# Token-major values in the gMLP and in the shared K/V, and a later start of FFN2's forms, in a one-core decoder step

## The chip, the cores and the metric

The kernel runs on one core of one Trainium2 chip, as one program. The metric is device time in microseconds: the median of three runs of the kernel before is 2067.21 us (2066.38 to 2067.87).

## The reference

One inference step of a two-layer decoder: 512 prompt tokens and 32 sample tokens (8 sequences of 4), model width 1024, everything in float32. Layer A mixes tokens with a gMLP, layer B with attention; the keys, the values and the forget gates of layer B come from layer A's output once ("shared K/V"). The parts that the change touches:

```python
def gmlp_mix(xn, w_in, v_norm, w_s, b_s, w_out):
    u, v = jnp.split(xn @ w_in, 2, axis=-1)
    v = rmsnorm(v, v_norm)
    ...
    s = jnp.einsum('gts,bnsgd->bntgd', ws, vg)      # per chunk of 128 tokens and group of 128 features
    s = s + b_s[:, :c].T[None, None, :, :, None]
    return (u * s) @ w_out, v                       # v of the sample tokens is an output

def shared_kv(h, kv_norm, w_kvf, b_f, k_norm):
    kvf = rmsnorm(h, kv_norm) @ w_kvf
    k = rmsnorm(kvf[..., :D_ATT].reshape(bsz, L, N_HEADS, HEAD_DIM), k_norm)
    v = kvf[..., D_ATT:2 * D_ATT].reshape(bsz, L, N_HEADS, HEAD_DIM)
    logf = jax.nn.log_sigmoid(kvf[..., 2 * D_ATT:] + b_f)
    return k, v, logf
```

Around these stand, in each layer, FFN1, the mixer, FFN2 and a gated per-layer embedding (PLE), each with its own rmsnorm and residual sum.

## The kernel before

Activations lie feature-major: a tile is 128 features by 544 tokens (512 of the prompt, then the 32 samples), eight such chunks make the width 1024. The order of the stages is FFN1, gMLP, FFN2, PLE, shared K/V, FFN1, attention, FFN2, PLE.

**Products.** float32 accuracy comes from fp32r matmuls: each operand is split into hi and lo, and three products are summed, hi·hi, hi·lo and lo·hi (L235, L239, L241 in `mm`, each in two matmuls of 256 and 288 columns). `tile_mm` makes one tile of 128 features by 544 tokens: the weights are the stationary operand, the activations the moving one, eight chunks of the contraction, 24 pairs of matmuls. Weights come in pieces of 512 KB in the order that `build` lists them: SP loads a piece (L159), ScalarE (ACT) casts it to hi (L192), VectorE (DVE) subtracts to get lo (L193), a few pieces ahead of their use. An activation is split in the same way by `prep` (L291 on ScalarE with the norm's gain, L292 on VectorE) or by `split_pair` (L279, L280). A norm's factor per token, rstd, is multiplied in after the product, when VectorE empties PSUM. A PSUM tile `ps` is two banks, and there are three; `pb` is one bank, and there are two. Each chunk of the residual that is complete calls `on_chunk`, which prepares the next stage's input (`next_norm`): the split, the sum of squares (a Square on ScalarE, L318, an add on GpSimd, L320), and, for the first pairs of chunks of a following FFN, `forms`, the sums and differences of blocks that the FFN's seven-product scheme multiplies (L301 twice on ScalarE; L305, L307, L308 on VectorE; two splits, L279 and L280). `early` says for how many pairs: 3 ahead of FFN2 of layer A, 2 ahead of FFN2 of layer B.

**gMLP.** Eight tiles of v are made feature-major, then eight of u. The spatial product wants v with tokens on the partitions, so `v_turn` multiplies by the norm and transposes a tile on TensorE (L612 four blocks of the prompt, L613 the samples) and ScalarE copies it back. `spatial` is plain fp32 (L623 the prompt, L626 the samples).

**Shared K/V** (`kv`). First the forget gates' tile, then eight tiles of k, then eight of v. A head's k norm needs the sum of squares over its 128 features: `head_stat` (L710) sums with a matmul of ones, heads 0 to 3 in one burst after head 5's tile and heads 4 to 7 in one burst after the first v tile; the chain of rsqrt follows on VectorE (L337, L340, L341), its rows go to DRAM (L721), come back to all partitions (`tmp<-rows`, L726), and `k_norm` (L784) multiplies. Each v tile is multiplied by rstd on VectorE (L765), stored, transposed on TensorE (L796, L797 in this stage's `v_turn`), split and written to DRAM for attention.

**Attention's end.** After the heads, the output is projected: first the tokens of the first half (`project_half`), then the second half, a chunk of 128 features at a time, with all eight heads in the contraction (`project`, L1172, L1175, L1176 in `product`; L1196 adds to the residual). Each of the eight `project` steps ends with `on_chunk`.

**Order.** The order within an engine is set by a scheduler from the program's order and the dependencies; in attention a list written by hand (`ORDER`) gives the program's order. ScalarE and VectorE run their instructions strictly in the order of their queue, and SP issues nearly all DMAs.

## Time and profile before

| | |
|---|---|
| median of 3 runs | 2067.21 us |
| the profiled execution | 2068.19 us |
| its span, first to last instruction | 2066.4 us |
| mean granted clock of TensorE | 0.999 |
| TensorE busy | 2042.8 us, 99% |
| VectorE busy | 1509.9 us, 73% |
| ScalarE busy | 941.1 us, 46% |
| GpSimd busy | 180.5 us, 9% |
| data moved | 237.94 MB, 115 GB/s on the mean |

A row of a timeline reads: start (us from the span's start), duration, engine, line, operation, the tile written and the tiles read, shape, how many instructions the row holds, and in brackets the idle time just before and what ended it. A matmul's duration includes its way through the array, so the pace of TensorE is read from one start to the next. A plain fp32 matmul leaves two records, an fp32r one leaves one.

### The profile page before, as it was taken

What the parts mean: (1) busy time and instruction counts of PE and PEld (TensorE: products, weight loads), DVE (VectorE), ACT (ScalarE), POOL (GpSimd) and SP (SyncE); (2) the same over time, 40 slices, a digit from 0 to 9 for tenths busy, and PEclk for the clock granted to TensorE, in tenths of its full rate; (3) what the DMA queues carried; (4) which work ended last, traced back from release to release, by engine and by line L of the source; (5) the groups of instructions that cost most, each with busy time, mean ns of one, the idle gap of its engine ahead of it and who ended that gap; (6) DMA issues with size and microseconds to landing.
All of it is one profiled execution on the core that took longest, in us unless ns stands there. A gap on an engine that the chain in (4) does not pass through costs nothing.

```text
span 2066.4 us, 38759 instructions
## 1 busy us (share of the span) xinstructions
PE 2042.8 (99%) x16388; PEld 2015.9 (98%) x16388; DVE 1509.9 (73%) x1874; ACT 941.1 (46%) x1389; POOL 180.5 (9%) x230
## 2 busy tenths in 40 slices
PE   8999999999999999999999999999999999999999
PEld 8999999999999999999999999999987999999999
DVE  7877777556687778776698777786476878777773
ACT  6535344423554344454356344444374744344451
POOL 0000000400100000052050000001042200000020
PEclk9999999999999999999999999999999999999999
DMA  5233234212223232432184322323668332232421
GB/s 184 83 111 110 74 105 146 92 45 82 83 92 113 72 113 79 147 98 92 35 321 168 102 103 93 113 74 121 214 209 287 103 103 82 103 103 82 129 97 44
DMA packets 93887, 237.94 MB, mean 115 GB/s; under 512 B 9602, under 2 KB 27554, under 8 KB 93714
## 3 DMA queue, kind: packets, MB, share of 16 engines
q1 hardware_dynamic: 93570, 235.42, 33.9%
q8 instruction: 129, 2.11, 0.4%
q14 instruction: 44, 0.36, 0.1%
q10 hardware_dynamic: 144, 0.04, 0.0%
HBM read 218.94 MB, written 16.49 MB: 114 GB/s over the span
## 4 chain that ended last, share of the span: by engine, by line
PE 93%; DVE 3%; DMA 1%; ACT 1%; issue 1%; POOL 1%; SPq 0%; ACTq 0%; DVEq 0%; POOLq 0%
PE ps L485 33%; PE ps L235 16%; PE ps L241 16%; PE ps L239 16%; PE pb L485 6%; PE ps L1172 1%; PE ps L1176 1%; DVE big L193 1%; PE ps L1175 1%; ACT big L192 0%; PE ps L1129 0%; DMA tmp<-rows 0%; PE ps L623 0%; PE pb L1091 0%; POOL big L837 0%
## 5 line engine op out<-in xcount | busy, mean ns | idle before, releaser
L485 PE MATMUL ps<-big,big 128*128 128x272 f32 x5616 | 727.2, 288 | 0.7 <-DVE big L502 0.7
L485 PEld LDWEIGHTS ps<-big,big 128*128 128x128 f32 x5616 | 714.2, 189 | 0.9 <-issue 0.9
L193 DVE TENSOR_TENSOR big<-big,big 128x1024 fp32r<-128x1024 f32 (+2 forms) x538 | 590.1, 1099 | 108.8 <-ACT big L192 108.2
L192 ACT CAST big<-big 128x1024 fp32r<-128x1024 f32 (+2 forms) x538 | 488.4, 932 | 265.1 <-DVE big L178 260.4
L235 PE MATMUL ps<-big,big 128*128 128x256 f32 (+1 forms) x2832 | 590.5, 290 | 8.0 <-ACT big L192 7.3
L241 PE MATMUL ps<-big,big 128*128 128x256 f32 (+1 forms) x2832 | 585.1, 288 | 1.0 <-DVE big L193 1.0
L239 PE MATMUL ps<-big,big 128*128 128x256 f32 (+1 forms) x2832 | 585.0, 287 | 0.0
L235 PEld LDWEIGHTS ps<-big,big 128*128 128x128 f32 x2832 | 454.1, 189 | 10.3 <-ACT big L192 7.3
L239 PEld LDWEIGHTS ps<-big,big 128*128 128x128 f32 x2832 | 457.1, 189 | 0.0
L241 PEld LDWEIGHTS ps<-big,big 128*128 128x128 f32 x2832 | 453.4, 188 | 2.5 <-DVE big L193 2.1
L320 POOL TENSOR_TENSOR st<-st,tmp 128x544 f32<-128x544 f32 (+1 forms) x63 | 88.3, 1401 | 1619.2 <-ACT tmp L318 1619.0
L524 DVE SCALAR_TENSOR_TENSOR big<-ps,big 128x544 f32<-128x544 f32 x160 | 115.6, 723 | 106.6 <-PE ps L241 106.4
L178 DVE TENSOR_TENSOR big<-big,big 128x1024 f32<-128x1024 f32 x156 | 190.1, 1219 | 0.0
L493 ACT COPY tmp<-ps 128x544 f32<-128x544 f32 x117 | 71.7, 613 | 147.4 <-PE ps L485 147.4
L448 ACT ACTIVATE big<-big 128x544 f32<-128x544 f32 x88 | 58.0, 660 | 161.9 <-DVE big L445 160.7
L485 PE MATMUL pb<-big,big 128*128 128x272 f32 x936 | 124.0, 288 | 0.0
L445 DVE TENSOR_TENSOR big<-big,st 128x1088 f32<-128x1088 f32 x88 | 113.4, 1290 | 10.6 <-ACT big L507 8.9
L485 PEld LDWEIGHTS pb<-big,big 128*128 128x128 f32 x936 | 120.2, 189 | 0.0
L291 ACT ACTIVATE big<-big,gains 128x544 fp32r<-128x544 f32 (+1 forms) x80 | 56.0, 704 | 119.0 <-DVE big L524 64.9
L280 DVE TENSOR_TENSOR big<-big,big 128x544 fp32r<-128x544 f32 (+1 forms) x104 | 75.2, 726 | 28.3 <-ACT big L279 28.0
L292 DVE SCALAR_TENSOR_TENSOR big<-big,gains,big 128x544 fp32r<-128x544 f32 (+1 forms) x80 | 63.9, 805 | 26.6 <-ACT big L291 26.6
L279 ACT CAST big<-big 128x544 fp32r<-128x544 f32 (+1 forms) x104 | 66.7, 645 | 29.0 <-DVE big L784 15.2
(187 smaller groups left out, 1246.2 us busy)
## 6 DMA issues: line engine op xcount, KB each, us to landing
big<-in_w SPq DMA_DIRECT2D x156, 512.0 KB
big<-in_w2a SPq DMA_DIRECT2D x64, 512.0 KB
big<-in_w2b SPq DMA_DIRECT2D x32, 384.0 KB
big<-in_w13p SPq DMA_DIRECT2D x16, 512.0 KB
big<-in_win SPq DMA_DIRECT2D x16, 512.0 KB
big<-in_wg SPq DMA_DIRECT2D x16, 512.0 KB
big<-in_wkv SPq DMA_DIRECT2D x16, 512.0 KB
big<-in_ck SPq DMA_DIRECT2D x16, 512.0 KB
```

What stands on the lines that cost most here:

```text
L178: self.nc.vector.tensor_tensor(t, a, b, ALU.add if op == "+" else ALU.subtract)
L192: self.nc.scalar.copy(hi, src)
L193: self.nc.vector.tensor_tensor(lo, src, hi.bitcast(F32), ALU.subtract)
L235: i = nc.tensor.matmul(out[:, a:b], wh, xh[:, a:b], start=s, stop=False)
L239: nc.tensor.matmul(out[:, a:b], wh, xl[:, a:b], start=False, stop=False)
L241: nc.tensor.matmul(out[:, a:b], wl, xh[:, a:b], start=False, stop=e)
L280: self.nc.vector.tensor_tensor(pair[:, 1, cols], src, pair[:, 0, cols].bitcast(F32), ALU.subtract)
L320: nc.gpsimd.tensor_tensor(acc[:, cols], acc[:, cols], sq, ALU.add)
L445: tt(g, g, rstd.unsqueeze(1).broadcast_to([P, 2, T]), ALU.mult)
L485: nc.tensor.matmul(dst[w], a[:, c], b, start=k in "152" and kp == 0 and n == 0, stop=kp == NKP - 1 and n == 2, skip_group_check=True)
L493: nc.scalar.copy(t["r" + k], t["C" if k == "5" else "A"])
L524: nc.vector.scalar_tensor_tensor(h[c], whole(out), 0.5, h[c], ALU.mult, ALU.add)
```

## The change

In the gMLP the prompt's v and in the shared K/V the prompt's v are made token-major at once. `token_half` takes a block of 128 tokens as the stationary operand and the weights' hi and lo as the moving one, 512 columns (features, four heads) at a time. The weights are laid out anew (`wgv`, `wv`): a piece is two chunks of the contraction by 512 features, four pieces make a half, and a piece is 4 blocks of tokens x 2 chunks x 3 products = 24 matmuls of 512 columns (L603, L604, L605). A half's result is two `ps` tiles, held over four pieces. The transposes on TensorE are gone.

The 32 sample tokens are done apart: `raw_sample` scales them by the gain, and plain fp32 matmuls with the raw weights (L611), four chunks of the contraction beside each other in 32 columns of the array each, give four partial sums stacked on the 128 partitions; `sample_sums` (L617) adds the four with one matmul of a 0/1 matrix. `columns` (L578, L580) turns rstd from a row into a column per token, eight small fp32 matmuls.

In the gMLP a half is copied out of PSUM by ScalarE, which also sums the squares; the norm's factor becomes a small column (`v_norm`), and VectorE multiplies it in. In the shared K/V ScalarE empties a half with rstd as its scale (L848, eight activations a half; L851 the samples'), and the steps of k, v, the statistics (L788), the norms (`k_norm`, now L896), the next stage's `prep` and `forms` follow a list, `KV_ORDER`. v's outputs change layout, and the host puts them back in order.

`early` becomes a map from the chunk after which `forms` runs to the pair: the same as before ahead of FFN2 of layer A, and ahead of FFN2 of layer B after chunks 5 and 6 instead of 1 and 3.

The lines of helpers move: L192, L193 become L198, L199; L279, L280 become L285, L286; L291, L292 become L297, L298; L305, L307, L308 become L311, L313, L314; L318 becomes L324; L337, L340, L341 become L343, L346, L347; L1196 becomes L1294.

VectorE in the shared K/V, around the end of the rsqrt chain of heads 4 to 7 (L341, L347). Before (L784 is the norm of heads 0 and 1, on `big_11000`, which L280 then splits; L877, L879, L880, L888 belong to the forget gates):

```order
L340 SCALAR_TENSOR_TENSOR tmp_11542<-pb_11532,tmp_11542 128x272
L877 TENSOR_SCALAR sm_12131<-sm_12044,consts 128x8
L280 TENSOR_TENSOR big_11560<-big_11000,big_11560 128x512
L341 SCALAR_TENSOR_TENSOR st_11541<-tmp_11542,st_11541 128x544
L879 SCALAR_TENSOR_TENSOR sm_12131<-sm_12044,consts,sm_12131 128x8
L292 SCALAR_TENSOR_TENSOR big_11566<-big_86,gains,big_11566 128x544
L879 SCALAR_TENSOR_TENSOR sm_12131<-sm_12044,consts,sm_12131 128x8
L193 TENSOR_TENSOR big_11570<-big_11399,big_11569 128x1024
L765 TENSOR_TENSOR tmp_11627<-ps_11578,st_10926 128x544
L784 SCALAR_TENSOR_TENSOR big_11000<-big_11000,gains,tmp_11462 128x544
```

Now (L896 is the norm, `big_11007` holds heads 4 and 5, `big_11208` heads 6 and 7):

```order
L343 SCALAR_TENSOR_TENSOR tmp_11312<-st_11311 128x544
L346 SCALAR_TENSOR_TENSOR tmp_11312<-pb_11301,tmp_11312 128x272
L346 SCALAR_TENSOR_TENSOR tmp_11312<-pb_11302,tmp_11312 128x272
L347 SCALAR_TENSOR_TENSOR st_11311<-tmp_11312,st_11311 128x544
L896 SCALAR_TENSOR_TENSOR big_11007<-big_11007,gains,tmp_11372 128x544
L896 SCALAR_TENSOR_TENSOR big_11007<-big_11007,gains,tmp_11374 128x544
L286 TENSOR_TENSOR big_11412<-big_11007,big_11412 128x512
L896 SCALAR_TENSOR_TENSOR big_11208<-big_11208,gains,tmp_11416 128x544
L298 SCALAR_TENSOR_TENSOR big_11418<-big_87,gains,big_11418 128x544
L896 SCALAR_TENSOR_TENSOR big_11208<-big_11208,gains,tmp_11476 128x544
L199 TENSOR_TENSOR big_11422<-big_11328,big_11421 128x1024
```

The norms of heads 4 to 7, which read the chain's rows back from DRAM into `tmp`, now stand right behind the chain; before, the norms of heads 1 to 3 stood between.

ScalarE at the same place now (L285 splits head 4, `big_11007`, L297 prepares a chunk for FFN1, L198 splits v's piece 5, L848 empties the first PSUM tile, `ps_11109`, of the first half of v):

```order
L285 CAST big_11412<-big_11007 128x512
L297 ACTIVATE big_11418<-big_87,gains 128x544
L198 CAST big_11421<-big_11328 128x1024
L848 ACTIVATE big_11458<-ps_11109,sm_10827 128x2x128
L848 ACTIVATE big_11459<-ps_11109,sm_10827 128x2x128
L848 ACTIVATE big_11458<-ps_11109,sm_10827 128x2x128
L848 ACTIVATE big_11459<-ps_11109,sm_10827 128x2x128
L848 ACTIVATE big_11458<-ps_11110,sm_10827 128x2x128
```

The split of piece 5 and the emptying of the first half stand behind the split of a head whose norm waits for the round trip.

ScalarE in attention's last projections. Before (L192 splits the weights of `project`, L301 and L279 belong to `forms`, L291 and L318 to `on_chunk`):

```order
L301 ACTIVATE big_18680<-big_86,gains 128x544
L291 ACTIVATE big_18473<-big_87,gains 128x272
L279 CAST big_18685<-tmp_18683 128x544
L318 ACTIVATE tmp_18728<-big_87 128x272
L279 CAST big_18686<-tmp_18684 128x544
L192 CAST big_18695<-big_18613 128x1024
L291 ACTIVATE big_18492<-big_87,gains 128x272
L318 ACTIVATE tmp_18765<-big_87 128x272
L192 CAST big_18732<-big_18648 128x1024
L301 ACTIVATE big_18768<-big_87,gains 128x544 x2
```

Now:

```order
L198 CAST big_18240<-big_18170 128x1024
L297 ACTIVATE big_17995<-big_87,gains 128x272
L324 ACTIVATE tmp_18236<-big_87 128x272
L198 CAST big_18277<-big_18207 128x1024
L198 CAST big_18314<-big_18244 128x1024
L297 ACTIVATE big_18014<-big_87,gains 128x272
L324 ACTIVATE tmp_18273<-big_87 128x272
L307 ACTIVATE big_18350<-big_86,gains 128x544 x2
```

The forms of pair 0 (L307 at the end) now stand behind the last weight splits of `project`.

The core of the diff:

```diff
+KV_ORDER = """
+k0 k1 c0 k2 k3 k4 s0 k5 r0 r1 v0 n0 r2 k6 n1 r3 k7 n2 p0 s1 v1 n3 p1 r4 r5 v2 n4 r6 p2 v3 n5 r7 p3 f0
+v4 n6 w0 p4 v5 n7 w0 p5 v6 f1 p6 v7 p7 w0 w0
+"""
...
-    def next_norm(self, h, gcol, early=0):
+    def next_norm(self, h, gcol, early={}):
...
-            if c % 2 and c // 2 < early and cols.stop == T:
-                box["f"].append(self.forms(h, gcol, c // 2, self.pairs(box)))
+            if c in early and cols.stop == T:
+                box["f"].append(self.forms(h, gcol, early[c], self.pairs(box)))
...
+    def raw_sample(self, h, gcol, x):
+        for c in range(NC_):
+            self.nc.gpsimd.tensor_scalar(x[:, c, :], h[c][:, SEQ:], self.gain(gcol + c), None, ALU.mult)
+        return x
+    def columns(self, rstd):
+        nc, t = self.nc, self.pb()
+        for j in range(4):
+            nc.tensor.matmul(t[:, j:j + 1], rstd[:, j * P:(j + 1) * P], self.ident[:, 0:1], start=True, stop=True)
+        for j in range(4):
+            nc.tensor.matmul(t[32 * j:32 * j + 32, 4:5], rstd[:, SEQ:], self.ident[:, 0:1], start=True, stop=True,
+                             skip_group_check=True)
+        rc = self.sm(5)
+        nc.scalar.copy(rc, t[:, 0:5])
+        return rc
+    def token_half(self, xs, xraw, half, u):
+        nc = self.nc
+        hi, lo = self.unit()
+        raw = self.raws[self.pieces[self.p_next - 1]["src"][0]]
+        self.advance()
+        if u == 0:
+            half["p"] = self.ps(), self.ps()
+            half["r"] = []
+        half["r"] += [raw[:, 0:512], raw[:, 512:1024]]
+        for i in range(4):
+            t, out = slice(i * P, i * P + P), half["p"][i // 2][:, i % 2, :]
+            for a in range(2):
+                k, c = 2 * u + a, slice(512 * a, 512 * a + 512)
+                xh, xl = xs[k]
+                nc.tensor.matmul(out, xh[:, t], hi[:, c], start=k == 0, stop=False)
+                nc.tensor.matmul(out, xh[:, t], lo[:, c], start=False, stop=False)
+                nc.tensor.matmul(out, xl[:, t], hi[:, c], start=False, stop=k == NC_ - 1)
+        if u % 2:
+            if u == 1:
+                half["s"] = self.pb()
+            for n in range(4):
+                k = 2 * u - 2 + n
+                nc.tensor.matmul(half["s"][32 * n:32 * n + 32, :], xraw[:, k, :], half["r"][k], start=k < 4, stop=k >= 4,
+                                 skip_group_check=True)
+    def sample_sums(self, sv, half):
+        t = self.pb()[:NS, :]
+        self.nc.tensor.matmul(t, self.c[:, C_SUM:C_SUM + NS], sv[:, 512 * half:512 * half + 512], start=True, stop=True)
+        return t
 
...
-        rstd, sq, v = None, self.st(), []
-        for c in range(NC_):
-            if rstd is None:
-                p, rstd = self.tile_rstd(xs, box["acc"])
-            else:
-                p = self.tile_mm(xs)
-            if c % 2 == 0:
-                vt = self.big()
-
-            def take(p=p, vc=vt[:, c % 2, :]):
-                nc.vector.tensor_tensor(vc, whole(p), rstd, ALU.mult)
-                self.ssq(sq, vc, first=not v)
-                v.append(vc)
-            self.evac(take)
+        gvr = self.big()[:, 0:2, :512]
+        nc.sync.dma_start(out=gvr[:NS], in_=i["gvrow"].partition_broadcast(NS).rearrange("p o (a n) -> p (o a) n", a=2))
+        xraw = self.raw_sample(h, G_MIX, self.ks)
+        ss, v, sv = self.sm(10), [], self.flat(1024)
+        nc.vector.memset(ss, 0.0)
+        for g in range(2):
+            half = {}
+            for u in range(4):
+                self.token_half(xs, xraw, half, u)
+                if (g, u) == (0, 1):
+                    rstd = self.rstd(box["acc"])
+                if (g, u) == (0, 3):
+                    rc = self.columns(rstd)
+            for a, p in enumerate(half["p"]):
+                x = self.flat(1024).rearrange("p (i d) -> p i d", i=2)
+                v.append(x)
+                nc.scalar.copy(x, p)
+                for n in range(2):
+                    k = 4 * a + 2 * n + g
+                    nc.scalar.activation(self.tmp()[:, :512], p[:, n, :], AF.Square, accum_out=ss[:, k:k + 1])
+            nc.scalar.copy(sv[:, 512 * g:512 * g + 512], half["s"])
...
-        def v_turn(c):
...
-            for j in range(4):
-                nc.tensor.transpose(t[:, 0, j * P:(j + 1) * P], v[c][:, j * P:(j + 1) * P], self.ident)
-            nc.tensor.transpose(t[:NS, 1, :P], v[c][:, SEQ:], self.ident)
...
+        def v_scale(g):
+            for a in range(2):
+                x, f = v[2 * g + a], rv[:, 2 * a:2 * a + 2]
+                nc.vector.tensor_tensor(x, x, f.unsqueeze(2).broadcast_to([P, 2, 512]), ALU.mult)
...
+        def v_step(n):
+            g, u = divmod(n, 4)
+            self.token_half(xs, xraw, half, u)
+            if u < 3:
+                return
+            rc = box["rc"]
+            vs = [self.flat(1024).rearrange("p (h i d) -> p h i d", h=2, i=4) for _ in range(2)]
+            for i in range(4):
+                for a in range(2):
+                    nc.scalar.activation(
+                        vs[a][:, :, i], half["p"][i // 2][:, i % 2, 256 * a:256 * a + 256].rearrange(
+                            "p (h d) -> p h d", h=2), AF.Copy, scale=rc[:, i:i + 1])
+            nc.scalar.activation(sv[:, 512 * g:512 * g + 512], half["s"], AF.Copy, scale=rc[:, 4:5])
+            box["v"] = [(4 * g + a, vs[a // 2][:, a % 2].rearrange("p i d -> p (i d)")) for a in range(4)]
...
+        def norm(hh):
+            with self.tc.issue_after(box["last"].ins):
                 self.k_norm(hh, kraw, rows)
...
+        do = dict(k=k_tile, v=v_step, w=v_store, c=cols, s=stats, r=row, n=norm, p=prep, f=forms)
+        for step in KV_ORDER.split():
+            do[step[0]](int(step[1:]))
...
-        on, nxt = self.next_norm(h, G_FFN2, early=3)
+        on, nxt = self.next_norm(h, G_FFN2, early={1: 0, 3: 1, 5: 2})
...
-        on, nxt = self.next_norm(h, G_FFN2 + 8, early=2)
+        on, nxt = self.next_norm(h, G_FFN2 + 8, early={5: 0, 6: 1})
```

More of the change, by code (lines that the diff above doesn't have):

```diff
@@ L646, in gmlp @@
         u_tile(0)
[L647 removed]
+        rv, vs = v_norm()
+        v_scale(0)
         u_tile(1)
+        sample_scale()
         u_tile(2)
[L650 to L654 removed]
+        for c, spatials in ((3, (0,)), (4, (1,)), (5, (2, 3)), (6, (4, 5)), (7, (6, 7))):
             u_tile(c)
[L656 to L657 removed]
+            if c == 3:
+                v_scale(1)
             spatial(*spatials)
@@ L743, in kv, with k_tile, take @@
         sqs, bcs, rows = [], [], {}
-        for hh in range(NH):
+        nxt = {"x": {}, "f": []}
+        box, half, sv = {}, {}, self.flat(1024)
+        xraw = self.small.tile([P, NC_ * NS], F32, tag="xraw", name="xraw", bufs=1)[:].rearrange("p (c t) -> p c t", t=NS)
+        self.raw_sample(h, G_KV, xraw)
+        def k_tile(hh):
             p = self.tile_mm(xs)
             if hh % 2 == 0:
-                kt = self.big()
-            def take(p=p, kc=kt[:, hh % 2, :]):
-                nc.vector.tensor_tensor(kc, whole(p), rstd, ALU.mult)
+                box["k"] = self.big()
+            def take(p=p, kc=box["k"][:, hh % 2, :]):
+                box["last"] = nc.vector.tensor_tensor(kc, whole(p), rstd, ALU.mult)
                 kraw.append(kc)
@@ L753, in kv @@
             self.evac(take)
-            if hh == 5:
-                bcs += self.head_rows(sqs[:4])
-            if hh >= 6:
-                rows[hh - 6] = bcs[hh - 6]()
-        vpend = None
-        nxt = {"x": {}, "f": []}
-        for hh in range(NH):
-            p = self.tile_mm(xs)
-            if hh == 0:
-                bcs += self.head_rows(sqs[4:])
-            vc = self.tmp()
-            last = nc.vector.tensor_tensor(vc, whole(p), rstd, ALU.mult)
-            nc.sync.dma_start(out=o["v"][hh], in_=vc)
-            if vpend is not None:
-                self.v_turn(*vpend)
-            vpend = (hh, vc)
-            with self.tc.issue_after(last.ins):
-                self.k_norm(hh, kraw, rows)
-            if hh + 2 < NH:
-                rows[hh + 2] = bcs[hh + 2]()
-            nxt["x"][hh] = self.prep(h[hh], ffn_gain + hh)
-            if hh in (3, 5):
-                nxt["f"].append(self.forms(h, ffn_gain, len(nxt["f"]), self.pairs(nxt)))
@@ new lines, in v_store, with cols, stats, row @@
+        def v_store(_):
+            for hh, x in box["v"][:2]:
+                pair = self.big(F32R)
+                nc.sync.dma_start(out=o["v"][hh], in_=x)
+                self.split_pair(pair, x, slice(0, SEQ))
+                nc.sync.dma_start(out=self.vd[hh], in_=pair[:, :, :SEQ].bitcast(F32))
+            del box["v"][:2]
+        def cols(_):
+            box["rc"] = self.columns(rstd)
+        def stats(a):
+            bcs.extend(self.head_rows(sqs[4 * a:4 * a + 4]))
+        def row(hh):
+            rows[hh] = bcs[hh]()
@@ L778, in kv @@
+        for a in range(2):
+            nc.scalar.copy(vs[:, a, :], self.sample_sums(sv, a))
+        nc.sync.dma_start(out=o["vs"].rearrange("t (a n) -> t a n", a=2), in_=vs)
+        nc.sync.dma_start(out=self.vsd[:].rearrange("t (a n) -> t a n", a=2), in_=vs)
         return nxt, rstd
@@ L1219, in build @@
         self.ffn_pieces(0)
-        plain([i["win"][NC_ + c] for c in range(NC_)] + [i["win"][c] for c in range(NC_)])
+        plain([i["wgv"][c] for c in range(NC_)] + [i["win"][c] for c in range(NC_)])
         plain(i["wout"][c] for c in range(NC_))
@@ L1223, in build @@
         ple_units(0)
-        plain([i["wf"]] + [i["wkv"][c] for c in range(2 * NC_)])
+        plain([i["wf"]] + [i["w" + x[0]][int(x[1])] for x in KV_ORDER.split() if x[0] in "kv"])
         self.ffn_pieces(2)
```

82 lines of the change are left out of this document (41 added, 41 removed).

## The prediction

> **What bounds the kernel now.** I read the page's busy times first, then the waits of TensorE, then timelines of the places that the change touches. The page's row on TensorE, and four rows of its waits (engine, line, what it waited for: us in total, times, longest):
>
> ```profile
> PE 2042.8 (99%) x16388; PEld 2015.9 (98%) x16388; DVE 1509.9 (73%) x1874; ACT 941.1 (46%) x1389; POOL 180.5 (9%) x230
> PE ps L235 <- ACT big L192: 7.3, 1, 7.3
> PE ps L241 <- DVE big L193: 1.0, 2, 0.5
> PE pb L797 <- DVE big L280: 0.5, 1, 0.5
> ```
>
> TensorE sets the end; 7.3 us of its idle time is the first weights' arrival, which nothing here touches. So the change is worth what it takes from TensorE's own work, plus the waits that it removes and makes. The sum is made against the profiled execution (2068.19 us, span 2066.4) and set on the median of the runs, 2067.21; 0.2%, about 4.1 us, is what a measurement of this kernel can tell from no change.
>
> **The products of the prompt.** A tile of eight chunks was 24 pairs of matmuls (256 and 288 columns); a token-major half is four pieces of 24 matmuls of 512 columns. A pair's pace stands between two L235 rows that are 168 pairs apart, the other's between the first and the last of five rows of attention, of which four matmuls of 512 columns lie between:
>
> ```profile
> 345.13 0.41 PE L235 MATMUL ps<-big,big 128*128 128x256 f32 x2
> ...
> 386.94 0.41 PE L235 MATMUL ps<-big,big 128*128 128x256 f32 x2
> 1514.90 0.40 PE L1012 MATMUL ps<-big,big 128*128 128x512 f32 x1
> ...
> 1515.83 0.27 PE L1020 MATMUL ps<-neg,identr 128*128 128x256 f32 x1
> ```
>
> 41.81 / 168 = 0.249 us for a pair, 0.93 / 4 = 0.2325 us for 512 columns. Each of the two stages (gMLP's v, the shared v) had 192 pairs, 47.8 us, and gets 192 matmuls, 44.6 us: together **-6.3**.
>
> **The transposes** go: eight groups of five in each stage.
>
> ```profile
> 446.95 0.60 PE L612 MATMUL ps<-consts,big 128*128 128x128 f32 x4
> 447.38 0.27 PE L613 MATMUL ps<-consts,big 128*32 128x128 f32 x1
> 447.49 0.60 PE L612 MATMUL ps<-consts,big 128*128 128x128 f32 x4
> ```
>
> 447.49 - 446.95 = 0.54 for five, so 16 x 0.54 = **-8.6**.
>
> **The 32 sample tokens** now cost plain fp32 matmuls of 512 columns, four beside each other in the columns of the array. The nearest work is the paged attention's L1129 (same shapes), one group alone and then two in a row:
>
> ```profile
> 1578.44 0.29 PE L1175 MATMUL ps<-big,big 128*128 128x272 f32 x1
> 1578.66 1.05 PE L1129 MATMUL ps<-big,tmp 128*32 128x512 f32 x4
> 1579.64 0.39 PE L1176 MATMUL ps<-big,big 128*128 128x272 f32 x1
> 1579.87 0.29 PE L1172 MATMUL ps<-big,big 128*128 128x272 f32 x1
> ...
> 1583.93 1.92 PE L1129 MATMUL ps<-big,tmp 128*32 128x512 f32 x16
> 1585.78 1.06 PE L1134 MATMUL ps<-big,tmp 32*32 32x512 f32 x8
> ```
>
> The neighbours of the first group are half a pair, 0.125 us, apart when nothing lies between; here 1.43 us hold two such steps, so a group alone takes 1.43 - 0.25 = 1.18 us. Eight instructions in a row leave 16 records (each fp32 instruction leaves two) and take 1.85, with 0.25 for going in and out 2.1. gMLP's order has four groups apart: 4.7. The shared KV's has 8, 6 and 2 instructions together: 2.1 + 2.1 + 1.2 = 5.4. Together **+10.1**. `sample_sums` (L617) has no row: one instruction of 512 columns alone. A group's four run beside each other, so I price a single one like a group; below that the bound is half. Two in a row in gMLP 2.0, two apart in KV 2.4: **+4.4** (2.2 to 4.4).
>
> **The columns of rstd** (L578, L580): four fp32 matmuls with a stationary of 128 columns and four of 32, each moving one column. The spatial products of 128 columns and the samples' of 32 bound them:
>
> ```profile
> 489.81 1.95 PE L623 MATMUL ps<-big,big 128*128 128x128 f32 x16
> 491.69 0.63 PE L626 MATMUL ps<-tmp,big 32*128 32x32 f32 x4
> 492.25 0.52 PE L235 MATMUL ps<-big,big 128*128 128x256 f32 x2
> ```
>
> 0.12 a record at most (1.88 / 16) and 0.14 with the way out included (0.56 / 4): 16 records are at most 1.9; I put them at 1.3, since one column streams nothing, and the lowest at 0.6. Twice: **+2.6** (1.2 to 3.8). The Trainium skill, "TensorEngine Tiling (Array Packing)", section Instruction Overhead, has a matmul of one column cost as much as one of 60, about 60 cycles; sixteen of them would be an estimated 0.4 us, and the sum 1.8 us lower. No run here shows a one-column matmul.
>
> **The heads' statistics.** Before, the sums of squares of heads 4 to 7 were one burst; the new order has four pairs, each between other products, since the k tiles of heads 5 to 7 now have v pieces between them. A single pair (attention) and the burst:
>
> ```profile
> 1475.66 0.28 PE L241 MATMUL ps<-big,big 128*128 128x256 f32 x1
> 1475.86 1.10 PE L710 MATMUL pb<-tmp,ones 128*32 128x272 f32 x4
> 1476.90 0.40 PE L241 MATMUL ps<-big,big 128*128 128x288 f32 x1
> ...
> 1030.42 0.41 PE L241 MATMUL ps<-big,big 128*128 128x256 f32 x2
> 1030.76 1.12 PE L710 MATMUL pb<-tmp,ones 128*32 128x272 f32 x16
> 1031.81 0.52 PE L235 MATMUL ps<-big,big 128*128 128x256 f32 x2
> ```
>
> Next to 0.125 us without it, the pair costs 1476.90 - 1475.66 - 0.125 = 1.11, the burst 1031.81 - 1030.42 - 0.25 = 1.14. So 4 x 1.11 - 1.14 = **+3.3**.
>
> **Waits of the shared KV.** The three of 0.5 us above (L241 twice, L797) lie in this stage, behind a VectorE that multiplied every v tile by rstd; that work is now ScalarE's, so **-1.5**. One wait is new. VectorE's order now has k_norm of head 4 (L896) right behind the end of the rsqrt chain of heads 4 to 7, and k_norm needs the chain's result after a round trip through DRAM. ScalarE's split of head 4 waits for it, and behind that, strictly in order, stand the split of weight piece v5 and the evacuation of the first half's v, whose PSUM tile TensorE wants. Attention shows the whole trip (DVE's L341 ends the chain, SP's L721 writes rows, its L726 reads them back, L964 is the norm); the row ahead is KV's own write:
>
> ```profile
> 1037.97 1.14 SPq L721 DMA_DIRECT2D rows<-st  x4
> ...
> 1479.18 0.73 DVE L341 SCALAR_TENSOR_TENSOR st<-tmp,st 128x544 f32<-128x544 f32 x1
> 1479.97 1.14 SPq L721 DMA_DIRECT2D rows<-st  x4
> 1487.01 0.78 DVE L964 SCALAR_TENSOR_TENSOR big<-big,gains,tmp 128x544 f32<-128x544 f32 x1
> 1489.45 0.78 DVE L964 SCALAR_TENSOR_TENSOR big<-big,gains,tmp 128x544 f32<-128x544 f32 x1 [0.28 <-DMA tmp<-rows]
> ```
>
> ScalarE's steps from the groups of instructions (count | busy us, mean ns):
>
> ```profile
> L192 ACT CAST big<-big 128x1024 fp32r<-128x1024 f32 x378 | 391.4, 1047 | 265.1 <-DVE big L178 260.4 <-PE pb L485 2.1 <-ACT big L192 0.5
> L291 ACT ACTIVATE big<-big,gains 128x544 fp32r<-128x544 f32 x64 | 47.8, 750 | 98.2 <-DVE big L524 64.9 <-DVE big L661 17.4 <-DVE big L696 11.6
> L279 ACT CAST big<-big 128x512 fp32r<-128x512 f32 x16 | 9.9, 619 | 18.8 <-DVE big L784 15.2 <-DVE big L964 3.5
> ```
>
> Count from the end of the last statistic. To the write: 3.1 us in attention (1476.90 to 1479.97), 6.2 in KV (1031.81 to 1037.97, with other work between); I take 4.5. From the write to the first norm 7.0 at most, to the last 9.5; I take 6.0, as head 4's read is first in the queue. k_norm 0.8, split 0.6, next chunk's L291 0.75, v5's split 1.05: 13.7; the evacuation's first four activations, half the split's columns each, estimated 0.42: 15.4. TensorE's order has before that point 37 matmuls of 512 columns (8.6) and two of the samples' bursts (4.2): 12.8. So it waits 15.4 - 12.8, about **+2.5** (0 to 6). Before, the norms of heads 1 to 3 stood between chain and norm.
>
> What that does to the clock: in attention's tail, below, waits of 2.19 and 0.75 us were followed by a clock of 0.66. The Trainium skill, "TensorE: Matmul & The Clock Gate", section Why this matters for your kernels, allows idle gaps of up to about 3 us before the clock halves; this trace halved it with no gap over 2.19. By the rule a wait of 2.5 us costs no clock; by the row it may cost the 1.65 us worked out below, which I leave to the upper end.
>
> **Attention's tail.** The third and the fourth of the last eight projections waited, since `forms` for FFN2's pairs 0 and 1 stood ahead of weight splits on ScalarE and VectorE:
>
> ```profile
> 1617.59 0.29 PE L1176 MATMUL ps<-big,big 128*128 128x272 f32 x1
> 1620.06 0.39 PE L1172 MATMUL ps<-big,big 128*128 128x272 f32 x1 [2.19 <-ACT big L192]
> 1621.32 0.56 PE L1176 MATMUL ps<-big,big 128*128 128x272 f32 x1 [0.75 <-DVE big L193]
> 1624.84 0.29 PE L1176 MATMUL ps<-big,big 128*128 128x272 f32 x1
> ```
>
> The stretch's busy times by engine (PE, PEld, DVE, ACT, POOL), then the granted clock:
>
> ```profile
> 1620.00:1625.00 5.00, 4.19 (x19) 3.98 (x20) 4.82 (x7) 3.63 (x7) 0.99 (x1) 0.66 0.25 93
> ```
>
> From 1617.59 to 1624.84 are 18 steps of 0.125, 2.25 us: 5.0 were lost, of which 1.65 to the clock (15 steps from 1621.32 took 3.52). With the forms after chunks 5 and 6 every split stands ahead of them, and this goes. Late next is FFN2's start: its second and fourth weight pieces' lo now stand behind forms on VectorE; I count 1.0 lost (0 to 4). **-4.0**.
>
> **Sum:** -6.3 - 8.6 + 10.1 + 4.4 + 2.6 + 3.3 - 1.5 + 2.5 - 4.0 = **+2.5**: 2070.7 for the profiled execution, 2069.7 on the median. gMLP's own part is about nothing (-3.2 - 4.3 + 4.7 + 2.0 + 1.3 = +0.5), KV's about +6, attention's -4. In gMLP no new wait is counted: the evacuation by ScalarE (46% busy) of a half lies under the next half's 22 us; uncovered, a copy like L192's 1.05 and two squares like L279's 0.62 would cost 2.3 us for each PSUM tile.
>
> **The rivals.** (a) Slower: the KV's wait grows. Between KV's reads and writes the trip can be longer than attention's; if k_norm of head 4 comes 9.5 us behind the write, as the last of the four did, the wait is 6.0, and 1.65 of clock come on top: 2069.7 + 3.5 + 1.65 = 2074.9. It decides from a trip of about 7.6 us on, since 1.6 us more than forecast pass the 0.2%. For it: the norm's own queue, and ScalarE in strict order. Against it: head 4's read stands first in the queue. (b) Faster: the trip is over in time (wait 0), the tail's gain is whole, the columns cost 0.6 each and a lone L617 half a group: 2069.7 - 2.5 - 1.0 - 1.4 - 2.2 = 2062.6. For it: a lone fp32 matmul and a one-column one have no row here; against it: the dependent order on VectorE. (c) FFN2's start takes back all that the tail gains (+4.0 on the forecast, 2073.7): the forms need both chunks of a pair, so five more VectorE steps a pair fall into the first tiles. For it: VectorE has 4.82 of 5.00 us busy in the row above; against it: eight splits less ahead of them.
>
> **How the numbers follow.** Forecast 2069.7, no change that can be told: 0.40, of its own 2066 to 2072. (a) 0.22, (b) 0.25, (c) 0.13. From (b) most is faster by over 0.2%, from (a) and (c) nearly all slower: faster 0.24, same 0.41, slower 0.35. The range, 2061.5 to 2075.5, takes in (b) and (a).
>
> **What would show it.** Right: in the changed kernel's profile L611 bursts at 1.2 and 2.1 us, L617 at 1.0 to 1.2, single statistics at 1.1; in KV, VectorE's L896 waiting for DMA and TensorE's first 512-column matmul on the reused PSUM tile waiting for ScalarE's L848, for 1 to 5 us; no wait and a full clock in the last projections. Wrong: 512-column matmuls at another pace than 0.23, or a new wait over 3 us in gMLP or FFN2's start.

## The result and the profile after

| | before | changed |
|---|---|---|
| median of 8 runs | 2068.2 us | 2073.36 us |
| range of the runs | 2066.38 to 2069.22 | 2071.69 to 2074.93 |
| span of the profiled execution | 2066.4 us | 2069.9 us |

The ratio is 1.0028, 95% interval 1.0019 to 1.0037: 5.2 us slower between the medians, 3.9 to 7.7 by the interval. The forecast was 2.5 us slower, with 2061.5 to 2075.5 as its range. The profiled execution of the changed kernel is its fastest of the eight (2071.69), which is why the spans differ by 3.5 only.

To see where the time went I cut TensorE's rows at places that both kernels have: the first and the last matmul of each FFN's seven-product scheme (L485 before, L491 now) and the last matmul of attention's projection (L1175 before, L1273 now). Microseconds between the cuts, in the two kernels and in three of the experiments below:

| stretch | before | changed | forms only | gMLP only | K/V only |
|---|---|---|---|---|---|
| end of FFN1's products to start of FFN2's, layer A: gMLP | 220.3 | 219.4 | 220.3 | 219.4 | 220.3 |
| end of FFN2's products of A to start of FFN1's of B: PLE, shared K/V | 232.8 | 240.3 | 232.9 | 232.9 | 240.0 |
| FFN1's products of B | 306.5 | 306.5 | 306.5 | 306.5 | 306.5 |
| to the last projection: attention | 223.1 | 217.4 | 217.1 | 225.2 | 223.8 |
| to the end of FFN2's products of B | 331.1 | 334.2 | 334.2 | 331.2 | 331.2 |

The four other stretches agree to 0.1 us wherever the code is the same, and the changed K/V to 0.3 (240.3 and 240.0). Attention's moves by 2.1 us here between kernels that share all of its code, and by 3.3 over the experiments (216.3 in e7, 219.5 in e6), so a difference there counts only above that. Part of it is the clock: the last projections of "gMLP only" have the waits of before (2.18 and 0.75 us), but the clock is halved behind them for 6.8 us, where before had 3.4, and that alone is 1.7 us. A row has the stretch, its length, the busy us of PE, PEld, DVE, ACT and POOL with the number of instructions, the granted clock, the DMA share and GB/s; here of the kernel before, then of "gMLP only":

```profile
1621.40:1624.80 3.40, 3.40 (x15) 3.40 (x16) 3.26 (x5) 2.23 (x4) 0.49 (x1) 0.50 0.02 7
1620.30:1627.10 6.80, 6.05 (x28) 5.93 (x27) 6.31 (x9) 5.35 (x8) 1.00 (x1) 0.50 0.11 43
```

The changed K/V costs 7.5 us, the changed gMLP gains 0.9, the moved forms gain 5.7 before FFN2 and lose 3.1 in it: 4.0 us slower by the stretches, in executions whose spans differ by 3.5.

**The shared K/V.** Three rows of the changed kernel's waits of TensorE (line, what it waited for: us in total, times, longest); before had 0.5 (L797) and 1.0 (L241) in this stage, and of the second row here two of the three times, 1.0 us, fall in it:

```profile
PE ps L603 <- ACT big L198: 2.5, 1, 2.5
PE ps L247 <- DVE big L199: 1.5, 3, 0.5
PE ps L603 <- ACT big L848: 1.0, 1, 1.0
```

The first and the third are the wait that was forecast, in its two parts: the split of v's piece 5, then the emptying of the first half's PSUM tile. Rows of the timeline of the place, in order of time, with those of other work left out:

```profile
1039.73 9.75 POOL L935 TENSOR_TENSOR big<-big 128x512 f32<-128x512 f32 x5
1043.11 0.40 PE L605 MATMUL ps<-big,big 128*128 128x512 f32 x1
1043.44 1.10 PE L788 MATMUL pb<-tmp,ones 128*32 128x272 f32 x4
1044.47 0.73 PE L603 MATMUL ps<-big,big 128*128 128x512 f32 x2
1046.02 2.31 DVE L199 TENSOR_TENSOR big<-big,big 128x1024 fp32r<-128x1024 f32 x1
1048.26 1.80 DVE L343 SCALAR_TENSOR_TENSOR tmp<-st 128x544 f32<-128x544 f32 x1
1051.00 0.73 DVE L347 SCALAR_TENSOR_TENSOR st<-tmp,st 128x544 f32<-128x544 f32 x1
1051.80 1.38 SPq L799 DMA_DIRECT2D rows<-st  x4
1055.06 1.91 PE L611 MATMUL pb<-big,xraw 128*32 128x512 f32 x12
1056.36 0.79 DVE L896 SCALAR_TENSOR_TENSOR big<-big,gains,tmp 128x544 f32<-128x544 f32 x1 [4.64 <-DMA tmp<-rows]
1057.18 0.62 ACT L285 CAST big<-big 128x512 fp32r<-128x512 f32 x1 [7.05 <-DVE big L896]
1058.36 1.03 ACT L198 CAST big<-big 128x1024 fp32r<-128x1024 f32 x1
1059.29 3.02 ACT L848 ACTIVATE big<-ps,sm 128x256 f32<-128x256 f32 x8
1059.44 0.49 PE L603 MATMUL ps<-big,big 128*128 128x512 f32 x1 [2.47 <-ACT big L198]
1060.90 0.50 PE L603 MATMUL ps<-big,big 128*128 128x512 f32 x1 [0.97 <-ACT big L848]
```

Read it from the last statistic, behind which the next matmul starts at 1044.47. The rsqrt chain ends at 1051.73 and the rows are written at 1051.80, 7.3 us later; head 4's norm (L896) starts at 1056.36, 4.6 us after the write. ScalarE has stood idle for 7.05 us before it splits that head, then come L297, piece 5's split and the emptying, and TensorE's two waits end behind these two. On VectorE L199 took 2.31 us, L343 1.80, while GpSimd was in the forget gates' running sums (L935, five instructions, 9.75 us). The clock after the waits, and the clock in attention's last projections (columns as above):

```profile
1060.00:1065.00 5.00, 4.10 (x12) 3.26 (x13) 4.86 (x6) 5.00 (x12) 3.36 (x3) 0.71 0.99 325
1065.00:1070.00 5.00, 5.00 (x22) 4.02 (x22) 4.57 (x7) 2.56 (x4) 2.98 (x3) 0.95 1.05 384
1620.00:1625.00 5.00, 5.00 (x42) 5.00 (x41) 5.00 (x7) 3.51 (x7) 0.87 (x2) 1.00 0.24 92
```

0.29 x 5 + 0.05 x 5 = 1.7 us were lost to a lowered clock in the shared K/V, and none is lost any more in the projections, where before had 0.66 and 19 matmuls in the same stretch. So the loss to the clock moved from one place to the other and stayed as large.

### The profile page after: what moved, and what is told of

Its sections match the earlier page's. It is cut to its first block, busy times and chain, and to the rows that moved or that the text cites. A ratio compares the mean times of both kernels' runs of the same rounds, so it can differ in the third digit from the quotient of the medians.

```text
span 2069.9 us, 37980 instructions
## 1 busy us (share of the span) xinstructions
PE 2045.3 (99%) x16024; PEld 1987.0 (96%) x16024; DVE 1501.3 (73%) x1850; ACT 948.0 (46%) x1405; POOL 188.2 (9%) x240
## 4 chain that ended last, share of the span: by engine, by line
PE 93%; DVE 3%; ACT 2%; issue 1%; DMA 1%; SPq 0%; POOL 0%; ACTq 0%; DVEq 0%
PE ps L491 33%; PE ps L241 15%; PE ps L247 15%; PE ps L245 15%; PE pb L491 5%; PE ps L603 1%; PE ps L605 1%; PE ps L604 1%; ACT big L198 1%; DVE big L199 1%; PE ps L1270 1%; PE ps L1274 1%; PE ps L1273 1%; DMA tmp<-rows 1%; PE ps L1227 0%
## 5 line engine op out<-in xcount | busy, mean ns | idle before, releaser
L491 PE MATMUL ps<-big,big 128*128 128x272 f32 x5616 | 727.7, 288 | 1.7 <-DVE big L508 1.2
L491 PEld LDWEIGHTS ps<-big,big 128*128 128x128 f32 x5616 | 714.2, 188 | 2.3 <-issue 1.6
L199 DVE TENSOR_TENSOR big<-big,big 128x1024 fp32r<-128x1024 f32 (+2 forms) x538 | 594.7, 1108 | 140.6 <-ACT big L198 139.9
L198 ACT CAST big<-big 128x1024 fp32r<-128x1024 f32 (+2 forms) x538 | 487.9, 932 | 267.5 <-DVE big L184 262.8
L241 PE MATMUL ps<-big,big 128*128 128x256 f32 (+1 forms) x2576 | 535.8, 289 | 7.8 <-ACT big L198 7.8
L247 PE MATMUL ps<-big,big 128*128 128x256 f32 (+1 forms) x2576 | 532.3, 288 | 1.5 <-DVE big L199 1.5
L245 PE MATMUL ps<-big,big 128*128 128x256 f32 (+1 forms) x2576 | 531.2, 287 | 0.0
L241 PEld LDWEIGHTS ps<-big,big 128*128 128x128 f32 x2576 | 413.0, 189 | 12.0 <-ACT big L198 8.2
L247 PEld LDWEIGHTS ps<-big,big 128*128 128x128 f32 x2576 | 412.1, 188 | 3.2 <-DVE big L199 2.7
L245 PEld LDWEIGHTS ps<-big,big 128*128 128x128 f32 x2576 | 414.6, 189 | 0.0
L326 POOL TENSOR_TENSOR st<-st,tmp 128x544 f32<-128x544 f32 (+1 forms) x56 | 77.8, 1389 | 1210.5 <-ACT tmp L324 1210.1
L491 PE MATMUL pb<-big,big 128*128 128x272 f32 x936 | 124.0, 288 | 0.0
L491 PEld LDWEIGHTS pb<-big,big 128*128 128x128 f32 x936 | 120.2, 188 | 0.0
L297 ACT ACTIVATE big<-big,gains 128x544 fp32r<-128x544 f32 (+1 forms) x80 | 56.0, 706 | 118.6 <-DVE big L530 64.9
L286 DVE TENSOR_TENSOR big<-big,big 128x544 fp32r<-128x544 f32 (+1 forms) x112 | 80.7, 728 | 27.0 <-ACT big L285 26.9
L298 DVE SCALAR_TENSOR_TENSOR big<-big,gains,big 128x544 fp32r<-128x544 f32 (+1 forms) x80 | 67.8, 853 | 28.7 <-ACT big L297 28.6
L285 ACT CAST big<-big 128x544 fp32r<-128x544 f32 (+1 forms) x112 | 71.0, 644 | 21.9 <-DVE big L896 8.9
```

The lines of the kernel that those rows point to most:

```text
L198: self.nc.scalar.copy(hi, src)
L199: self.nc.vector.tensor_tensor(lo, src, hi.bitcast(F32), ALU.subtract)
L241: i = nc.tensor.matmul(out[:, a:b], wh, xh[:, a:b], start=s, stop=False)
L245: nc.tensor.matmul(out[:, a:b], wh, xl[:, a:b], start=False, stop=False)
L247: nc.tensor.matmul(out[:, a:b], wl, xh[:, a:b], start=False, stop=e)
L286: self.nc.vector.tensor_tensor(pair[:, 1, cols], src, pair[:, 0, cols].bitcast(F32), ALU.subtract)
```

## The experiments

### One part at a time

The runs are called e1 to e11 in the order in which they stand. The first three kernels each take one part of the change into the kernel before; the fourth is the changed kernel with the old K/V.

Forms only, on the kernel before:

```diff
-        on, nxt = self.next_norm(h, G_FFN2 + 8, early=2)
+        on, nxt = self.next_norm(h, G_FFN2 + 8, early={5: 0, 6: 1})
```

gMLP only, on the kernel before (with the changed `gmlp` and its output):

```diff
-        plain([i["win"][NC_ + c] for c in range(NC_)] + [i["win"][c] for c in range(NC_)])
+        plain([i["wgv"][c] for c in range(NC_)] + [i["win"][c] for c in range(NC_)])
```

K/V only, on the kernel before (with the changed `kv` and its outputs); e4 is the changed kernel with this undone:

```diff
-        plain([i["wf"]] + [i["wkv"][c] for c in range(2 * NC_)])
+        plain([i["wf"]] + [i["w" + x[0]][int(x[1])] for x in KV_ORDER.split() if x[0] in "kv"])
```

> The kernel before with the moved forms alone (pairs 0 and 1 of FFN2 of layer B after chunks 5 and 6 of the projection). Theory: the tail gains 5.0 to 5.7 us and FFN2's start gives back 2.3 to 3.0, as in the changed kernel's trace, so 2.0 to 3.5 us faster, with waits on VectorE's lo splits at FFN2's start and none in the last projections. Rival: what FFN2's start gives back belongs to the other parts' buffers and not to the forms, and the whole 5 to 6 us stay.

Measured 2065.39 us against 2068.34, ratio 0.9987 (0.9978 to 0.9996). TensorE's rows with a wait from the last projections to FFN2's first tiles are two:

```profile
1634.72 0.52 PE L235 MATMUL ps<-big,big 128*128 128x256 f32 x2 [0.23 <-ACT big L192]
1635.98 0.52 PE L241 MATMUL ps<-big,big 128*128 128x256 f32 x2 [0.49 <-DVE big L193]
```

The waits of 2.19 and 0.75 us in the last projections are gone, and FFN2's stretch gives back 3.1 us (334.2), here too, without the other parts. The rival falls.

> The changed gMLP alone, shared K/V and forms as before. Theory: the stage is 1.0 us shorter (the trace's 219.4 against 220.4 us from the end of FFN1's products to the start of FFN2's), the kernel 0.5 to 1.5 us faster. Rival: the prediction's sum, 0.5 us slower, with the trace's difference a matter of the run.

Measured 2068.77 us against 2068.34, ratio 1.0001 (0.9992 to 1.0010). The time can't tell the two apart; the stage can: 219.4 us in every kernel with the new gMLP, 220.3 in every one without. It gains 0.9, close to the theory's 1.0.

> The changed shared K/V alone, gMLP and forms as before. Theory: 7 to 9 us slower: about 3.5 us of waits behind the norm of head 4, 1.7 of lowered clock, the rest TensorE's own added work; the clock falls below 0.9 in some 5 us there. Rival: the wait is an accident of when the stage before ends, and without the other parts it is gone: 2 to 4 us slower.

Measured 2075.95 us against 2068.34, ratio 1.0037 (1.0023 to 1.0050): 7.6 us slower. The two waits at L603 are there again, 2.42 and 0.96 us, so they do not depend on the other parts.

> The changed kernel with the shared K/V as before (new gMLP and moved forms stay). Theory: the parts add, so 3 to 4.5 us faster than the kernel before. Rival: the gains of the tail and of the gMLP are not there without the new K/V, and the time is that of the kernel before within 1 us.

Measured 2067.37 us against 2068.34, ratio 0.9996 (0.9987 to 1.0005): 1 us faster, with an interval from 2.7 faster to 1 slower. The sum of the parts would be 2.5 faster by the times (e1's 2.95 less e2's 0.4). Attention's stretch was 218.9 here and 217.1 in e1 with the same code, which is the difference. The total thus tells the theory from its rival no more than it tells this kernel from the one before; by the stretches the parts add (219.4 in the gMLP, 334.2 in FFN2).

### What sets the wait in the shared K/V

> The changed kernel with the norms of heads 4 to 7 behind the first half's emptying in the list of steps, so that on ScalarE the split of v's piece 5 and the eight activations that empty the first half stand ahead of head 4's split. Theory: the waits of 2.5 and 1.0 us and the 1.7 us of lowered clock go, the samples' products fall into one more group apart (about +1), so about 4 us less than the changed kernel, 0 to 2 us over the kernel before. Rival: what costs is TensorE's own added work and the wait only moves to another buffer; 4 to 6 us over the kernel before, as changed.

```diff
-k0 ... k7 n2 p0 s1 v1 n3 p1 r4 r5 v2 n4 r6 p2 v3 n5 r7 p3 f0
-v4 n6 w0 p4 v5 n7 w0 p5 v6 f1 p6 v7 p7 w0 w0
+k0 ... k7 n2 p0 s1 v1 n3 p1 r4 r5 v2 r6 p2 v3 r7 p3 v4 n4 n5
+n6 w0 p4 v5 n7 w0 p5 f0 v6 f1 p6 v7 p7 w0 w0
```

Measured 2071.48 us against 2068.09, ratio 1.0017 (1.0008 to 1.0026): 3.4 over the kernel before, where the changed one was 5.2 over it. The wait at L603 is gone and the clock there is 1.00. But the work that was put later (norms, forms) now stands at FFN1's first tile (a row of TensorE, then the busy times and the clock behind it):

```profile
1095.42 0.52 PE L241 MATMUL ps<-big,big 128*128 128x256 f32 x2 [2.50 <-ACT big L198]
```

```profile
1098.00:1101.00 3.00, 3.00 (x18) 3.00 (x18) 2.82 (x5) 2.97 (x4) 0.00 (x0) 0.63 0.97 373
```

ScalarE is in order there too: the forms' L307 and L285 stand ahead of FFN1's weight split. So theory and rival hold in part: the wait was head 4's norm, and it moved. The stage is 239.5 us instead of 240.3, and of the 4 us that the theory counted on the medians show 1.8.

> The changed kernel with GpSimd's running sums of the forget gates eight steps later in the background work; ScalarE's order around the wait stays as changed (head 4's split first). Theory: the wait is long because the chain is late: VectorE's instructions took about twice their time (L199 2.08 and 2.31 us where 1.22 is usual) while GpSimd was busy 9.2 of 10 us beside them. With GpSimd elsewhere the write comes 3 to 4 us earlier, TensorE's wait falls under 0.5 us and the clock stays; 4 to 5 us less than the changed kernel, 0 to 1.5 us over the kernel before. Rival: the trip through DRAM and the norms behind it set the wait; it stays over 2 us, and the time stays 4 to 6 us over the kernel before.

```diff
+        for _ in range(8):
+            yield
         pool = nc.gpsimd
         w = [self.big()[:].rearrange("p a b -> p (a b)") for _ in range(2)]
```

Measured 2081.95 us against 2068.09, ratio 1.0065 (1.0051 to 1.0079): 13.9 us slower, where 0 to 1.5 was expected. At the place the theory was right. VectorE's and SP's rows, and the first of FFN1's tiles:

```profile
1043.98 1.22 DVE L199 TENSOR_TENSOR big<-big,big 128x1024 fp32r<-128x1024 f32 x1
1047.85 0.72 DVE L347 SCALAR_TENSOR_TENSOR st<-tmp,st 128x544 f32<-128x544 f32 x1
1048.64 1.11 SPq L799 DMA_DIRECT2D rows<-st  x4
...
1097.58 0.82 PE L241 MATMUL ps<-big,big 128*128 128x256 f32 x2 [5.34 <-ACT big L198]
```

Without GpSimd beside it L199 takes 1.22 us instead of 2.31, and the rows are written at 1048.64. Counted from the matmul behind the last statistic (1045.56 here), that is 3.1 us instead of 7.3. No wait is left at L603, and the clock there is 1.00. What I had not priced is what the postponed work does later (the edit postpones all of the forget gates' work from these sums on): it meets FFN1's first tiles, where TensorE waits 5.34 us, and further on a gate of FFN1 (6.3 us in one wait for VectorE), with the clock at 0.51 for 6.9 us at each of the two places. That FFN's products take 314.5 us instead of 306.5.

> The changed kernel with the statistics of heads 4 to 7 held together in one burst, the last head first. Theory: four single pairs at 1.1 us become one burst at 1.1, 3.2 us less of TensorE's work, while the wait behind head 4's norm stays as it is counted from the burst; 1.5 to 2.5 us over the kernel before. Rival: the three early heads' single pairs lay where TensorE had time, or the wait grows by as much as the work shrinks; 4 to 6 us over the kernel before.

```diff
-            for j, sq in enumerate(sqs):
-                self.nc.tensor.matmul(...)
+            for j, sq in list(enumerate(sqs))[::-1]:
+                i = self.nc.tensor.matmul(...)
+                if pin:                                  # in the shared K/V
+                    self.tc.keep_in_program_order(i)
```

Measured 2066.99 us against 2068.09, ratio 0.9992 (0.9983 to 1.0001). The four single pairs are one burst, and the wait is as it was (L850 is the emptying here):

```profile
1040.37 1.12 PE L788 MATMUL pb<-tmp,ones 128*32 128x272 f32 x16
1056.81 0.50 PE L603 MATMUL ps<-big,big 128*128 128x512 f32 x1 [2.58 <-ACT big L198]
1058.28 0.50 PE L603 MATMUL ps<-big,big 128*128 128x512 f32 x1 [0.96 <-ACT big L850]
```

The stage falls by 3.6 us, from 240.3 to 236.7, close to the 3.2 of work taken out. The kernel is 1.1 us faster than the one before by the medians, with an interval that takes in no change, where the theory had it 1.5 to 2.5 slower; the rest of the difference to the changed kernel lies in attention's stretch (216.3) and elsewhere, within what moves from kernel to kernel.

> Both the later norms and the one burst in the changed kernel. Theory: the two savings add, some 7 us less than the changed kernel, 1 to 3 us faster than the kernel before. Rival: one of them covers the other, not faster than the kernel before.

Both edits together: 2065.82 us against 2068.09, ratio 0.9989 (0.9980 to 0.9998), 2.3 us faster. The stage is 235.1 us, still 2.3 over the old K/V; a wait of 2.42 us stands at FFN1's first tiles, as in e5.

### Where the forms stand

These two have the new gMLP and the old K/V, and another map.

```diff
-        on, nxt = self.next_norm(h, G_FFN2 + 8, early={5: 0, 6: 1})
+        on, nxt = self.next_norm(h, G_FFN2 + 8, early={3: 0, 5: 1})     # e9
+        on, nxt = self.next_norm(h, G_FFN2 + 8, early={4: 0, 6: 1})     # e10
```

> New gMLP, shared K/V as before, and the forms of pairs 0 and 1 after chunks 3 and 5 of the last projection (changed: 5 and 6; before: 1 and 3). Theory: what FFN2's start gives back (334.2 us from the last projection to the end of its products, against 331.1) is the forms of pair 1 falling into its first tiles; two chunks earlier, 1 to 3 us of it come back, while five weight splits still stand ahead of the first forms on ScalarE and the last projections stay without a wait over 0.5 us: 3 to 6 us faster than the kernel before. Rival: the tail is only free of waits when all eight splits are ahead, and what FFN2's start gains is lost there: 0 to 2 us faster.

Measured 2066.36 us against 2067.81, ratio 0.9993 (0.9984 to 1.0002). FFN2's stretch is 334.7 us; nothing came back. Its first tile waits, and the clock falls behind it:

```profile
1630.77 0.52 PE L241 MATMUL ps<-big,big 128*128 128x256 f32 x2 [1.34 <-ACT big L198]
1631.72 0.52 PE L241 MATMUL ps<-big,big 128*128 128x256 f32 x2 [0.18 <-ACT big L198]
```

```profile
1632.00:1635.00 3.00, 3.00 (x18) 3.00 (x18) 2.96 (x5) 1.77 (x5) 1.34 (x1) 0.61 0.34 138
```

The weight split that ends this wait stands on ScalarE directly behind the last split of a block of forms (L285), which itself waited for VectorE's part of them (L314):

```profile
1629.13 0.65 ACT L285 CAST big<-tmp 128x544 fp32r<-128x544 f32 x1 [0.19 <-DVE tmp L314]
1629.68 1.99 ACT L198 CAST big<-big 128x1024 fp32r<-128x1024 f32 x2
```

The last projections kept no wait over 0.27 us, so not all eight splits have to be ahead of the forms; but the time is the rival's, 1.5 us less than before with an interval that takes in no change.

> As the run with the forms after chunks 3 and 5, but after chunks 4 and 6. Theory: between that and the changed map, FFN2's start at 332.5 to 334 us, 2 to 4 us faster than the kernel before. Rival: the give-back does not depend on where the forms stand by a chunk, 334.2 us, 1 to 2 us faster.

Measured 2065.30 us against 2067.81, ratio 0.9987 (0.9978 to 0.9996). FFN2's stretch is 331.9 us, 2.3 of the 3.1 are back, and neither of the two waits of FFN2's first tiles is left. So the give-back does depend on the place by a chunk, but earlier is not better. My reading is that it counts which weight split stands directly behind a block of forms; no run tries that by itself. This kernel is 2.5 us faster than the one before (0.8 to 4.5 by the interval); e1 (2.95) and e8 (2.3) can't be told from it.

### The sample tokens' price

> The changed kernel with only the first half of the contraction for the sample tokens' v in the gMLP and in the shared K/V (one group of four L611 matmuls a half instead of two; the other four chunks are left out). Theory: a group apart costs 1.0 to 1.2 us, so the gMLP's stage falls from 219.4 to 217.0 to 217.4 us; in the shared K/V the two long bursts halve, 1.9 us less. Rival: the groups run beside other products and cost little: the gMLP's stage stays over 218.5 us.

```diff
-        if u % 2:
-            if u == 1:
-                half["s"] = self.pb()
+        if u == 1:
+            half["s"] = self.pb()
             for n in range(4):
```

Measured 2069.30 us against 2067.81, ratio 1.0007 (0.9998 to 1.0017). The gMLP's stage fell to 216.9 us: 2.5 for two groups, so 1.25 a group. The shared K/V's fell by 1.2 us only, to 239.1, and its rows say why (the samples' line is L610 here):

```profile
1050.47 1.07 PE L610 MATMUL pb<-big,xraw 128*32 128x512 f32 x8
1052.13 1.07 PE L610 MATMUL pb<-big,xraw 128*32 128x512 f32 x8
1057.97 0.79 PE L603 MATMUL ps<-big,big 128*128 128x512 f32 x1 [4.78 <-ACT big L198]
```

The two bursts are 0.8 us shorter each than the 1.9 of the full ones, and the wait behind them is 4.78 us instead of 2.47. TensorE comes earlier and waits longer: counted from the matmul behind the last statistic, the wait ends after 15.6 us here and after 15.0 in the changed kernel, so the end of that place is set by the chain through DRAM, VectorE and ScalarE. Behind the longer wait the clock is at 0.51 for 6.9 us, where the changed kernel had 0.51 for 3.5. It follows that the wait is real and not a share of TensorE's own work.

## Why the prediction was right, and where it was not

The forecast's sign and range hold, and its mechanism in the shared K/V is what happened. It gave most weight to a change that can't be told from none; the interval says it can, by 3.9 us at least, and the 5.2 us between the medians are twice the 2.5 forecast. That the sum came as near as it did is in part luck: gMLP came out 1.4 us below its share, the shared K/V 1.5 above and the forms 1.4 above, and inside the shared K/V two larger errors stood against each other. By its own steps:

**The prices of TensorE's work** were right where a row stood near. The changed gMLP has a group of samples alone, `columns`, and the two sums in a row:

```profile
402.51 0.40 PE L605 MATMUL ps<-big,big 128*128 128x512 f32 x1
402.84 1.06 PE L611 MATMUL pb<-big,ks 128*32 128x512 f32 x8
403.84 0.50 PE L603 MATMUL ps<-big,big 128*128 128x512 f32 x1
...
418.78 0.95 PE L578 MATMUL pb<-consts,st 128*128 128x1 f32 x8
419.66 0.24 PE L580 MATMUL pb<-consts,st 128*32 128x1 f32 x8
419.83 0.50 PE L603 MATMUL ps<-big,big 128*128 128x512 f32 x1
...
435.73 0.41 PE L247 MATMUL ps<-big,big 128*128 128x256 f32 x2
436.07 1.90 PE L617 MATMUL pb<-big,consts 128*32 128x512 f32 x4
437.90 0.52 PE L241 MATMUL ps<-big,big 128*128 128x256 f32 x2
```

403.84 - 402.51 - 0.2325 = 1.10 for a group, and the first matmul behind it runs 0.1 late (forecast 1.18; by e11 1.25). `columns` takes 419.83 - 418.78 = 1.05 (1.3). Two sums take 437.90 - 435.73 - 0.25 = 1.92 (2.0). A lone statistic pair takes 1044.47 - 1043.11 - 0.2325 = 1.13 (1.11), by the rows from the shared K/V above. The 16 records of `columns` take 66 ns each on the mean; the eight with a stationary of 128 columns take 0.11 us each, about the pace of L623's 128 columns. One column is thus priced far above what the Trainium skill's "TensorEngine Tiling (Array Packing)", section Instruction Overhead, makes of it, an estimated 25 ns for sixty cycles.

**gMLP** was forecast at +0.5 and came to -0.9. The prices above are a little lower than forecast, and the stage has eight records of the rsqrt sum's matmul (L362) instead of twelve (L356), about 0.5 us by their starts, which the sum had left out. I have not shown that these are all of the 1.4 us.

**The shared K/V** was forecast at about +6 and came to +7.5, out of two errors against each other. TensorE's own work: of 240.3 us, waits take 4.6 by the profile's rows (2.47 and 0.97 at L603, and 0.17, 0.49 and 0.48 at FFN1's first tiles) and the clock 1.7; before had 2.2 of waits in 232.8, one of them, 0.70, in PLE. That leaves 234.0 against 230.6, +3.4, where the sum had +5.0. One reason shows in the rows: the last samples' matmuls and a sum's run at the same time, in other columns of the array:

```profile
1070.44 0.40 PE L605 MATMUL ps<-big,big 128*128 128x512 f32 x1
1070.78 0.62 PE L611 MATMUL pb<-big,xraw 128*32 128x512 f32 x2
1070.79 0.62 PE L617 MATMUL pb<-big,consts 128*32 128x512 f32 x1
...
1071.77 0.73 PE L603 MATMUL ps<-big,big 128*128 128x512 f32 x2
1072.62 1.05 PE L617 MATMUL pb<-big,consts 128*32 128x512 f32 x2
1073.59 0.50 PE L604 MATMUL ps<-big,big 128*128 128x512 f32 x1
```

The last group and the first sum take 1071.77 - 1070.44 - 0.2325 = 1.10 together, the second sum 1073.59 - 1071.77 - 2 x 0.2325 = 1.35: 2.45, where the sum had 1.2 + 2.4 = 3.6. I have not taken the rest, some 0.4 us, apart.

The waits and the clock were the larger part: 4.6 + 1.7 - 2.2 = +4.1, where the sum had -1.5 + 2.5 = +1.0. "-1.5" for the three old ones was mostly wrong, by a reading of the place: only the wait of L797 stood among the v tiles, and it is gone. The two of L241 stood at FFN1's first tiles already before (1079.64 and 1099.25 us, where v's last tile had ended at 1078), behind weight splits of VectorE that the change leaves there, and two of 0.5 us stand there still (L247, above; its third is at FFN2's start in layer B), with 0.17 behind a hi split. The new wait, "about +2.5", was 3.4 in the two rows. The step that failed is "to the write ... I take 4.5": it took 7.3, since GpSimd's running sums fell beside VectorE's chain, which the sum had no term for; e6 shows it, with 3.1 us to the write when GpSimd is elsewhere. The trip that follows, 4.6 us, was shorter than the 6.0 taken, which hid part of that. The Trainium skill, "SBUF — State Buffer", section SBUF: two separate sides, says that a VectorE instruction with two SBUF inputs and a GpSimd instruction that reads SBUF shut each other out for a whole instruction; L199 with two inputs at 2.31 us beside GpSimd and 1.22 without agrees.

The clock, 1.7 us, I had left to the upper end. No gap in the changed K/V was longer than 2.47 us, and the clock was halved, as the row from attention had it. The rule of the Trainium skill's "TensorE: Matmul & The Clock Gate", section Why this matters for your kernels, which asks to avoid idle gaps of over about 3 us, would have let these pass and does not suffice here.

**Attention's tail** gained the 5.0 that was forecast: its two waits are gone and the clock is full (5.7 in the stretch, where attention's own moves are of 2 us). "FFN2's start: I count 1.0 lost" was 3.1, within its 0 to 4; e1 shows that it belongs to the forms alone, e10 that one chunk decides over 2.3 of it.

Of the rivals, (a) is the nearest to what happened: a longer wait and a lower clock, though the trip was not the cause; (c) held in part, as FFN2's start took back 3.1 of the 5.0 that the tail gained and not all of it; of (b) only the price of the shared K/V's two sums came, 2.45 with the last group where 3.6 had been counted.

## What to carry to other kernels

A result that goes through DRAM and back should have other work behind it in the queue of every in-order engine that needs it; look in the order of the engine that splits weights and empties PSUM for what stands behind the consumer, and count what GpSimd does beside the producer. Before work is moved off a wait, find what it meets at the new place: e5, e6 and e9 each removed a wait and left or made another one, and work that is taken from TensorE between the start of such a chain and its wait (e11) lengthens the wait, while work taken from ahead of the chain's start counts in full (e7, 3.6 us of the stage). Small fp32 matmuls that run beside each other in columns of the array are cheap together and dear one by one: four statistics cost 1.1 us in a burst and 1.1 us each alone.
